# Head sums of an RWKV-7 layer: two rounded passes for one fp32 pass, and what moves with them

## The chip, the cores and the metric

The kernel runs on one core of a Trainium2 chip. The metric is the device time of one execution in microseconds (us), the median of the runs. TensorE (PE) multiplies, VectorE (DVE) and ScalarE (ACT) do the elementwise work, GpSimd (POOL) a little of it, and SyncE (SP) starts most of the DMA transfers.

## The reference

One layer of a hybrid decoder step: 1024 prompt tokens and 8 x 8 sample tokens, 1088 columns in all, model width 1024. `w_in` projects to RWKV-7 columns (14 blocks of 128), pooling columns (4 blocks) and gates (16 blocks). The sums over the 64 channels of a head are the three that the change touches:

```python
xl = pr + (pr_prev - pr) * lp["mu_shift"]                       # token shift
r, k, v, xw, xa, xg = jnp.split(xl, RWKV_SPLITS, axis=-1)
...
kk = heads(k * lp["k_k"])
kk = kk * lax.rsqrt(jnp.sum(kk * kk, axis=-1, keepdims=True) + 1e-12)
...
y, wkv_new = wkv7_scan(wkv_prev.astype(f32), rh, heads(decay), kh, vh, kk, ah)
mean = jnp.mean(y, axis=-1, keepdims=True)
var = jnp.mean(jnp.square(y - mean), axis=-1, keepdims=True)
y = ((y - mean) * lax.rsqrt(var + GN_EPS)).reshape(B, T, MIX_WIDTH)
y = y * lp["ln_w"].astype(f32) + lp["ln_b"].astype(f32)
bonus = jnp.sum(rh * kh * lp["r_k"].astype(f32), axis=-1, keepdims=True) * vh
y = (y + bonus.reshape(B, T, MIX_WIDTH)).astype(pr.dtype) * g
```

Then follow the causal pooling branch, the gated merge, `w_out`, and a squared-ReLU MLP (1024 to 4096 and back) between two adaptive norms.

## The kernel before

Channels lie on the 128 partitions, the 1088 tokens along the free dimension, cut in chunks (364, 362, 362 columns, or 512, 288, 288). The big products are done with a value split in two rounded halves (type fp32r): `hi` is a rounded copy made by ACT, `lo` the rest, subtracted by DVE, and three passes replace one fp32 product (`whi` and `wlo` are the halves of a weight, `hx` those of the activations). The small products of the heads are plain fp32.

The work of TensorE is one list, written out by hand when the program is built. `Pace.run` keeps an estimated TensorE clock. The stream `back` gives the weight products of the projection, a job for each block of `w_in`. The streams `fore` (chains of the state, heads, pools, the branch product's rows) are generators; each `yield n` says that its next step is to be put n estimated nanoseconds later, and until then products of `back` are put in between. The other engines' lists are made by a scheduler from the same program. Every engine runs its list in order. PSUM tag `w` has two banks used in turn, `mm` four, `wc` two; the SBUF ring `wt` has five buffers.

For each of four pairs of heads f (called head 0 to 3 here), `heads` runs: `front(f)` with the sample tokens of head f-1 beside it (`both` alternates two generators); `scores(f)`, in which the bonus follows the first unit; then `inverse`, `level` and `affine` (the 64 x 64 triangular inverse of each chunk) with `post(f-1)` beside them. At the end come `sample(3)` and `post(3)`.

- `front` squares k (ACT, L570), sums the squares over a head with a block matrix of ones (`kc("bones")`, an fp32 product in tag `w`), takes the inverse root in `rinv` (Sqrt on ACT at L332, reciprocals on DVE at L334 in pieces of at most 182 columns), and then the two decay products, each read by a Tanh (L582, L585). DVE does the rest (L602 to L627), and step by step the recurrent state S (L899).
- `scores` copies diagonal blocks with ACT (`iv`, L702).
- `post` is the group norm: a mean sum, its subtraction (L1004), a square (L1005), a second sum, `rinv`, scale and bias (L1011), bonus and gate (L1012, L1013). A gate product and its copy (L997) come first.
- `level` copies the products of the triangle from PSUM with DVE (L797, L808) and ACT (L812).
- `rwkv_cols` is the projection job of an RWKV block; its token shift is two DVE passes over the tile (L450, L452) and one over the sample tokens (L454). `gate` applies a Tanh to gate blocks (L471).
- The pool jobs add up windows with DVE (L508 to L521); `pools` multiplies the result by a 128 x 128 matrix (`plw`) and splits it (L548 on ACT, L549 on DVE).

An activation of another table set than the last is preceded by an ACT_TABLE_LOAD; Sqrt and Tanh are in different sets.

Of the kernel before, what the change touches and what calls it, by code (L numbers as in the profile page):

```python
# [18 lines left out]
P = 128  # L19
# [3 lines left out]
TS = 8  # L23
# [20 lines left out]
for _name, _w in (("ident", 128), ("ones", 128), ("bones", 128), ("strict", 64), ("incl", 64), ("strict8", 64), ("incl8", 64),  # L44
                  ("qm", 8), ("icnt", 16), ("one0", 9), ("par", 2), ("m16", 32), ("i32", 32), ("sel", 18)):
    KC[_name] = (_n, _w)
    _n += _w
# [3 lines left out]
def const_table():  # L51
    t = np.zeros((P, NKC), np.float32)

    def put(name, a):
        o, w = KC[name]
        t[:, o:o + w] = a

    r = np.arange(P)[:, None]
    put("ident", np.eye(P))
    put("ones", 1.0)  # L60
# [64 lines left out]
class K:  # L125
# [209 lines left out]

    def modulate(self, h, xn, g, am, kb, c0=0, n=NT, o=0):
# [87 lines left out]
    def rwkv_cols(self, b, act=None, tags=("mm", "mm", "mm")):  # L424
# [19 lines left out]
        def after():  # L444
# [5 lines left out]
            nc.vector.tensor_tensor(d[:, :1096], px[:, :1096], px[:, 1:1097], op=ALU.subtract)  # L450
            mu = self.par("mu", b)
            nc.vector.scalar_tensor_tensor(d[:, :NPR], d[:, :NPR], mu, px[:, 1:1 + NPR], op0=ALU.mult, op1=ALU.add)  # L452
            dv = d[:, 1025:1097].rearrange("p (q t) -> p q t", t=9)
            nc.vector.scalar_tensor_tensor(s.rearrange("p (q t) -> p q t", t=TS), dv[:, :, 0:8], mu, pv[:, :, 1:9],  # L454
# [76 lines left out]
    def pools(self):  # L531
# [3 lines left out]
        for g in range(4):  # L535
# [3 lines left out]
            yield 6500 + 1300 * g  # L539
# [16 lines left out]
    def front(self, f):  # L556
# [14 lines left out]
        t1, tha = self.wt(), self.wt()  # L571
        yield 8000 if f else 13000

        for c0, n in FP:
            ps = self.ps("w")
            self.mm(ps[:, :n], self.kc("bones"), kk[:, c0:c0 + n], start=True, stop=True)
            self.rinv(ps, n, kk[:, c0:c0 + n], 1.0, 1)
            yield 800
        for c0, n in FP:
# [19 lines left out]
        for c0, n in FH:  # L599
# [3 lines left out]
            nc.vector.tensor_tensor_scan(t, self.kscan[:, s], t, 0.0, ALU.mult, ALU.add)  # L603
# [19 lines left out]
        yield X(8 + f)  # L623
        v = self.wt()
        nc.sync.dma_start(v, self.d_x[8 + f])
        q = self.wt()
        nc.vector.scalar_tensor_tensor(q, r, self.par("r_k", f), k, op0=ALU.mult, op1=ALU.mult)  # L627
# [16 lines left out]
    def scores(self, f, d):  # L644
# [4 lines left out]
        yield from self.bonus(f, d)  # L649
# [3 lines left out]
    def bonus(self, f, d):  # L653

        nc, q, v, bv = self.nc, d["q"], d["v"], self.wt()
# [318 lines left out]
    def post(self, f):  # L974
# [9 lines left out]
        g2 = self.sm.tile([P, P], F32, tag="sw", bufs=2, name=self.nm("sw"))  # L984
        nc.sync.dma_start(g2, self.io["g2"][:, fs])
        sq = self.wt()
        bv = self.wt()
        nc.sync.dma_start(bv, self.d_bv[f])
        sg = self.wt()
        nc.sync.dma_start(sg, self.d_x[13])  # L990
        if not last:
            yield 5000

        for c0, n in CH:
            ps = self.ps("w")
            self.mm(ps[:, :n], g2, sg[:, c0:c0 + n], start=True, stop=True)
            nc.scalar.activation(sg[:, c0:c0 + n], ps[:, :n], AF.Copy)  # L997
            yield 500
# [29 lines left out]
        else:  # L1028
            live = [[piece(c0, n), self.pace.t + 700 * i] for i, (c0, n) in enumerate(CH)]
# [10 lines left out]
            hi, lo = self.row(self.p1, "wt", 5, F32R), self.row(self.p1, "wt", 5, F32R)  # L1040
            nc.scalar.activation(hi, y, AF.Copy)
            nc.vector.tensor_tensor(lo, y, hi.bitcast(F32), op=ALU.subtract)
# [4 lines left out]
    def heads(self):  # L1047

        for f in range(4):
# [8 lines left out]
            fill = self.post(f - 1) if f else self.ada_fill()  # L1058
            self.ds[f] = d

# [5 lines left out]
            yield from self.both(main(), fill)  # L1066
# [31 lines left out]
    def run(self):  # L1098
        tc, nc, io = self.tc, self.nc, self.io
        with ExitStack() as ctx:  # L1100
# [20 lines left out]
            nc.vector.tensor_scalar(self.hp[:, 12:16], self.hp[:, 8:12], -1.0, 1.0, op0=ALU.mult, op1=ALU.add)  # L1121
            self.sst = self.cp.tile([P, 14, 8], F32, name="sst")
# [21 lines left out]
    def phase1(self, ctx):  # L1144
# [27 lines left out]
        self.kscan = sm.tile([P, NT], BF16, name="kscan")  # L1172
        nc.gpsimd.memset(self.kscan, 1.0)
        nc.gpsimd.memset(self.kscan[:, 0:NPR:64], 0.0)
        nc.gpsimd.memset(self.kscan[:, NPR:NT:8], 0.0)
# [58 lines left out]
    def phase2(self):  # L1234
# [76 lines left out]
        gt = self.cp.tile([P, 8, 9], F32, name="gt1")  # L1311
        g2 = self.cp.tile([P, 8, 9], F32, name="g2")
# [460 lines left out]
    def residual(self, x, gt):  # L1773
        nc = self.nc

        def consume(c0, n, ps):
            m = min(n, NPR - c0)
            nc.vector.scalar_tensor_tensor(x[:, c0:c0 + m], ps[:, :m], gt[:, 0:1], x[:, c0:c0 + m], op0=ALU.mult, op1=ALU.add)
            if m < n:
                t = self.cp.tile([P, 64], F32, tag="rs", bufs=2, name=self.nm("rs"))  # L1780
# [109 lines left out]
```

## Time and profile before

| | |
|---|---|
| timed runs | 1677.7, 1677.36, 1667.94 us; median 1677.36 us |
| profiled execution | 1670.78 us, span 1669.0 us, mean granted clock 0.987 |
| PE, DVE, ACT, POOL busy | 1590.6, 1097.5, 638.2, 138.7 us |
| instructions | 35468 |
| heads and projections | about 60 to 812 us; merge and MLP after that |

A row of the timeline has the start, the length, engine, line, operation and operands, how many instructions are drawn together, and in brackets the idle time before them with what ended it. A row of grouped instructions has the shapes, the count, busy time, mean length in nanoseconds, idle time before and its causes. A row by stretch has for each engine busy time and count, then the granted TensorE clock, the DMA share and GB/s. In the waits stand total, times and longest.

### The profile page before, as it was taken

The page shows a single profiled execution, that of the slowest core. Times are in us where ns is not written, and L with a number is a line of the kernel's source. Part 1 is how long each engine was busy: PE and PEld are TensorE (multiplying, and loading weights), DVE is VectorE, ACT ScalarE, POOL GpSimd, SP SyncE. Part 2 cuts the span into 40 slices and gives each one's busy share as a digit, 9 for nine tenths or more (in the row PEclk, how much of TensorE's full clock was granted, in tenths as well). Part 3 has the DMA queues.
Part 4 walks back from the last instruction along what each step waited for, and adds up shares of the span by engine and source line. Part 5 has one row for each costly group of instructions (what it writes and reads, how often), then busy time and mean ns, then how long its engine had stood idle before and what let it go on. Part 6 is the DMA issues. An engine that isn't in the chain of part 4 may idle for free.

```text
span 1669.0 us, 35468 instructions
## 1 busy us (share of the span) xinstructions
PE 1590.6 (95%) x14619; PEld 1477.6 (89%) x14619; DVE 1097.5 (66%) x1911; ACT 638.2 (38%) x1249; POOL 138.7 (8%) x199
## 2 busy tenths in 40 slices
PE   4989999989897999999999999999999999999997
PEld 2878887887786879888999999999999999999997
DVE  4685658573859283824654479799866887566775
ACT  4443333343334333432222356222233434433651
POOL 0100101000000000000250130000000032000000
PEclk9999998999999999999999999999999999999999
DMA  9233312323241324175687456566434997665663
GB/s 350 81 101 137 137 60 78 116 77 113 88 137 44 134 75 147 54 276 180 220 307 274 150 182 217 184 236 212 161 141 151 364 365 256 200 212 163 213 197 121
DMA packets 121858, 288.37 MB, mean 173 GB/s; under 512 B 21120, under 2 KB 26752, under 8 KB 121696
## 3 DMA queue, kind: packets, MB, share of 16 engines
q1 hardware_dynamic: 113312, 264.65, 45.7%
q10 hardware_dynamic: 8240, 20.95, 3.6%
q8 instruction: 115, 1.88, 0.4%
q0 software_dynamic: 144, 0.51, 0.1%
q14 instruction: 47, 0.39, 0.1%
HBM read 208.77 MB, written 77.28 MB: 171 GB/s over the span
## 4 chain that ended last, share of the span: by engine, by line
PE 53%; DVE 6%; DMA 6%; issue 1%; ACT 1%; POOL 0%; SPq 0%; ACTq 0%; DVEq 0%; POOLq 0%
PE mm L156 36%; PE wc L156 10%; PE w L156 7%; DMA hid<-in_w_ff 1%; DVE wt L334 1%; DMA t<-d_t 1%; DMA mg<-in_w_ff 1%; DMA d_t<-hx 1%; DMA hid<-in_w_ada_mlp 1%; DVE wlo L1231 0%; DMA t<-d_th 0%; DVE hx L1582 0%; DVE hx L1466 0%; DMA wraw<-in_w_br 0%; DVE wlo L176 0%
## 5 line engine op out<-in xcount | busy, mean ns | idle before, releaser
L156 PE MATMUL mm<-hx,whi 128*128 128x362 f32 (+2 forms) x2944 | 708.5, 328 | 4.2 <-ACT px L471 1.5
L156 PEld LDWEIGHTS mm<-hx,whi 128*128 128x128 f32 x2944 | 499.7, 191 | 48.1 <-issue 22.1
L156 PE MATMUL mm<-hx,wlo 128*128 128x362 f32 (+2 forms) x1472 | 465.3, 316 | 1.8 <-DVE wlo L176 1.8
L156 PEld LDWEIGHTS mm<-hx,wlo 128*128 128x128 f32 x1472 | 281.0, 191 | 2.1 <-DVE wlo L176 2.1
L156 PE MATMUL mm<-mg,whi 128*128 128x272 f32 (+2 forms) x1312 | 248.8, 288 | 0.5 <-DVE t L1463 0.5
L156 PEld LDWEIGHTS mm<-mg,whi 128*128 128x128 f32 x1312 | 205.5, 188 | 5.1 <-issue 2.5
L156 PE MATMUL mm<-mg,wlo 128*128 128x272 f32 (+2 forms) x656 | 188.8, 288 | 0.0
L156 PE MATMUL wc<-hx,whi 128*128 128x272 f32 x896 | 169.5, 287 | 0.0
L156 PEld LDWEIGHTS wc<-hx,whi 128*128 128x128 f32 x896 | 140.3, 188 | 0.1
L1230 ACT ACTIVATE whi<-hid 128x512 fp32r<-128x512 f32 x128 | 80.4, 630 | 142.7 <-PE mm L156 59.6
L176 DVE TENSOR_TENSOR wlo<-wraw,whi 128x512 fp32r<-128x512 f32 x84 | 59.9, 714 | 113.5 <-ACT whi L175 109.5
L156 PE MATMUL wc<-hx,wlo 128*128 128x272 f32 x448 | 129.1, 288 | 1.1 <-DVE wlo L1231 1.1
L156 PEld LDWEIGHTS mm<-mg,wlo 128*128 128x128 f32 x656 | 123.5, 188 | 0.0
L1231 DVE TENSOR_TENSOR wlo<-hid,whi 128x512 fp32r<-128x512 f32 x128 | 88.0, 688 | 46.4 <-ACT whi L1230 45.7
L175 ACT ACTIVATE whi<-wraw 128x512 fp32r<-128x512 f32 x100 | 62.8, 629 | 138.8 <-PE mm L156 80.8
L156 PE MATMUL w<-hx,whi 128*128 128x272 f32 (+1 forms) x480 | 96.3, 295 | 0.0
L156 PEld LDWEIGHTS wc<-hx,wlo 128*128 128x128 f32 x448 | 84.3, 188 | 1.5 <-DVE wlo L1231 1.5
L1783 POOL TENSOR_TENSOR hx<-hx,rs 128x64 f32<-128x64 f32 x24 | 35.1, 1464 | 566.2 <-DMA mg<-in_w_ff 378.5
L156 PEld LDWEIGHTS mm<-mg,hx 128*128 128x128 f32 x576 | 72.7, 188 | 5.0 <-issue 5.0
L156 PEld LDWEIGHTS w<-hx,whi 128*128 128x128 f32 x480 | 77.0, 188 | 0.0
L156 PE MATMUL mm<-mg,hx 128*128 128x272 f32 (+2 forms) x576 | 75.4, 290 | 0.0
L156 PE MATMUL w<-hx,wlo 128*128 128x272 f32 (+1 forms) x240 | 70.9, 295 | 0.3 <-DVE wlo L1231 0.3
(324 smaller groups left out, 2350.0 us busy)
## 6 DMA issues: line engine op xcount, KB each, us to landing
t<-d_t SPq DMA_DIRECT2D x56, 544.0 KB, 4.7
hid<-in_w_ff SPq DMA_DIRECT2D x110, 256.0 KB, 3.7
d_t<-hx SPq DMA_DIRECT2D x102, 272.0 KB, 2.2
hid<-in_w_ff SPq DMA_DIRECT2D x42, 512.0 KB, 4.0
wraw<-in_w_in SPq DMA_DIRECT2D x68, 256.0 KB, 2.8
mg<-in_w_ff SPq DMA_DIRECT2D x58, 256.0 KB, 5.4
hid<-in_w_ada_mlp SPq DMA_DIRECT2D x24, 512.0 KB, 5.8
d_th<-px SPq DMA_DIRECT2D x22, 544.0 KB, 3.0
```

The lines of the kernel that those rows point to most:

```text
L156: return self.nc.tensor.matmul(out, lhsT, rhs, **kw)
L175: nc.scalar.activation(hi, raw, AF.Copy)
L176: (nc.gpsimd if n % 2 and n >= self.solo else nc.vector).tensor_tensor(lo, raw, hi.bitcast(F32), op=ALU.subtract)
L334: nc.vector.reciprocal(out[:, a:min(a + 182, n)], out[:, a:min(a + 182, n)])
L1230: self.nc.scalar.activation(hi, src, AF.Copy)
L1231: (eng or self.nc.vector).tensor_tensor(lo, src, hi.bitcast(F32), op=ALU.subtract)
L1783: nc.gpsimd.tensor_tensor(x[:, NPR:NT], x[:, NPR:NT], t, op=ALU.add)
```

## The change

- `halves` splits a value in hi (ACT copy) and lo (DVE subtract); `sums` adds up both with a rounded block matrix `bones`, in two fp32r passes. They replace the fp32 sums of kk and bonus for all heads and of the group norms of heads 0 to 2. `post(3)` keeps its fp32 sums.
- The kk sums stand 2000 estimated nanoseconds later.
- The bonus leaves `scores` and runs beside `inverse`, ahead of the post of the head before.
- In posts 0 to 2 the gate products come behind the sums, and bonus and gate are applied to the whole tile.
- The token shift is `px * mu + (1 - mu) * shifted`: a scaled copy on ACT for the second term and one DVE pass.
- The pools' waiting times are 6000 + 1000 g for 6500 + 1300 g. Constants and buffers not needed go (`ones`, half of `kscan`), and three small tiles of the second phase move to another pool.

```diff
+    def halves(self, src, hi, lo):
+        self.nc.scalar.activation(hi, src, AF.Copy)
+        self.nc.vector.tensor_tensor(lo, src, hi.bitcast(F32), op=ALU.subtract)
+
+    def sums(self, hi, lo):
+        ps = self.ps("w")[:, :hi.shape[1]]
+        for i, x in enumerate((hi, lo)):
+            self.mm(ps, self.bones, x, start=i == 0, stop=i == 1)
+        return ps
...
-            nc.vector.tensor_tensor(d[:, :1096], px[:, :1096], px[:, 1:1097], op=ALU.subtract)
-            nc.vector.scalar_tensor_tensor(d[:, :NPR], d[:, :NPR], mu, px[:, 1:1 + NPR], op0=ALU.mult, op1=ALU.add)
+            nc.scalar.activation(d[:, :1096], px[:, 1:1097], AF.Copy, scale=self.mu1[:, b:b + 1])
+            nc.vector.scalar_tensor_tensor(d[:, :NPR], px[:, :NPR], mu, d[:, :NPR], op0=ALU.mult, op1=ALU.add)
...
-            yield 6500 + 1300 * g
+            yield 6000 + 1000 * g
...
-        t1, tha = self.wt(), self.wt()
-        yield 8000 if f else 13000
+        hi, lo = (self.row(self.p1, "wt", 5, F32R) for _ in range(2))
+        for c0, n in FH:
+            self.halves(kk[:, c0:c0 + n], hi[:, c0:c0 + n], lo[:, c0:c0 + n])
+        yield 10000 if f else 15000
         for c0, n in FP:
-            ps = self.ps("w")
-            self.mm(ps[:, :n], self.kc("bones"), kk[:, c0:c0 + n], start=True, stop=True)
-            self.rinv(ps, n, kk[:, c0:c0 + n], 1.0, 1)
+            self.rinv(self.sums(hi[:, c0:c0 + n], lo[:, c0:c0 + n]), n, kk[:, c0:c0 + n], 1.0, 1)
             yield 800
...
         yield from self.unit(f, d, 0)
-        yield from self.bonus(f, d)
         yield from self.unit(f, d, 2)
...
-            ps = self.ps("w")
-            self.mm(ps[:, :n], self.kc("bones"), q[:, c0:c0 + n], start=True, stop=True)
-            nc.vector.tensor_tensor(bv[:, c0:c0 + n], ps[:, :n], v[:, c0:c0 + n], op=ALU.mult)
+            s = slice(c0, c0 + n)
+            nc.vector.tensor_tensor(bv[:, s], self.sums(hi[:, s], lo[:, s]), v[:, s], op=ALU.mult)
...
+            def part(c0, n):
+                s = slice(c0, c0 + n)
+                self.halves(y[:, s], hi[:, s], lo[:, s])
+                yield 2500
+                nc.vector.scalar_tensor_tensor(y[:, s], self.sums(hi[:, s], lo[:, s]), -1.0 / 64, y[:, s], op0=ALU.mult, op1=ALU.add)
+                nc.scalar.activation(sq[:, s], y[:, s], AF.Square)
+                self.halves(sq[:, s], hi[:, s], lo[:, s])
+                yield 5500
+                self.rinv(self.sums(hi[:, s], lo[:, s]), n, sq[:, s], 1.0 / 64, 2)
+                nc.vector.tensor_tensor(y[:, s], y[:, s], sq[:, s], op=ALU.mult)
+                nc.scalar.activation(y[:, s], y[:, s], AF.Identity, bias=self.par("ln_b", f), scale=self.par("ln_w", f))
...
+            bv, sg = yield from gate()
+            nc.vector.tensor_tensor(y, y, bv, op=ALU.add)
+            nc.vector.tensor_tensor(y, y, sg, op=ALU.mult)
...
-            fill = self.post(f - 1) if f else self.ada_fill()
+            def fill():
+                yield from self.bonus(f, d)
+                yield from self.post(f - 1) if f else self.ada_fill()
```

Line numbers shift by the edit: L332 becomes L331, L334 L333, L471 L482, L582 L595, L797 L809, L808 L820, L508 L519, L910 L922, L1004 L1052, L1010 L1057.

The first place is ACT's list in the front of head 3, from the Sqrt of the first kk sum to the first decay Tanh (`px` are gate blocks, `y` sample rows). Before:

```order
L332 ACT_TABLE_LOAD
L332 ACTIVATE wt_6177<-w_6254,eps 128x512
L332 ACTIVATE wt_6177<-w_6269,eps 128x288
L332 ACTIVATE wt_6177<-w_6280,eps 128x288
L910 ACTIVATE y_6303<-wc_6019 128x256
L582 ACT_TABLE_LOAD
L582 ACTIVATE wt_6181<-w_6294,hp 128x512
```

Of the change (without the rows ahead and the tanhs behind):

```order
L331 ACT_TABLE_LOAD
L331 ACTIVATE wt_6181<-w_6277,eps 128x512
L482 ACT_TABLE_LOAD
L482 ACTIVATE px_6120<-mm_6121 128x364
L482 ACTIVATE px_6120<-mm_6122 128x362
L922 ACTIVATE y_6334<-wc_6021 128x256
L331 ACT_TABLE_LOAD
L331 ACTIVATE wt_6181<-w_6296,eps 128x288
L174 ACTIVATE whi_6307<-wraw_6305 128x512
L482 ACT_TABLE_LOAD
L482 ACTIVATE px_6120<-mm_6123 128x362
L331 ACT_TABLE_LOAD
```

Gate tanhs now stand between the Sqrts, each with a load, and one more Sqrt, a copy and a load follow before the first decay Tanh.

The second place is DVE's list in `post(1)`, beside `inverse` and `level` of head 2, around the reciprocals of the second sum (`hv` are products of the triangle, `px` and `d` pool 3's tiles). Before:

```order
L518 SCALAR_TENSOR_TENSOR px_5286<-px_5465,px_5286 128x1024
L334 RECIPROCAL wt_5372<-wt_5372 128x182 x2
L519 COPY px_5286<-zf_5478 128x15
L797 TENSOR_TENSOR hv_5629<-w_5564,kct 128x512
L334 RECIPROCAL wt_5372<-wt_5372 128x182
L334 RECIPROCAL wt_5372<-wt_5372 128x180
L1010 TENSOR_TENSOR wt_5368<-wt_5368,wt_5372 128x364
L334 RECIPROCAL wt_5372<-wt_5372 128x182
L334 RECIPROCAL wt_5372<-wt_5372 128x180
L1010 TENSOR_TENSOR wt_5368<-wt_5368,wt_5372 128x362
L549 SCALAR_TENSOR_TENSOR px_5465<-w_5655,part,d_5464 128x364
```

Of the change:

```order
L338 TENSOR_TENSOR wt_5404<-wt_5402,wt_5403 128x362 x2
L809 TENSOR_TENSOR hv_5597<-w_5532,kct 128x512
L333 RECIPROCAL wt_5402<-wt_5402 128x182 x3
L333 RECIPROCAL wt_5402<-wt_5402 128x180
L333 RECIPROCAL wt_5402<-wt_5402 128x182
L333 RECIPROCAL wt_5402<-wt_5402 128x180
L1057 TENSOR_TENSOR wt_5400<-wt_5400,wt_5402 128x364
L1057 TENSOR_TENSOR wt_5400<-wt_5400,wt_5402 128x362
L820 COPY hv_5739<-w_5642 32x512 x2
L1057 TENSOR_TENSOR wt_5400<-wt_5400,wt_5402 128x362
L175 TENSOR_TENSOR wlo_5755<-wraw_5752,whi_5754 128x512
L519 TENSOR_TENSOR d_5766<-px_5418 128x1038
```

The first product's step stands ahead of all reciprocals instead of behind two; the copy of the second comes behind all six; the pool's adds, which before came ahead of this piece, begin behind it.

More of the change, by code (lines that the diff above doesn't have):

```diff
@@ L1039, in post @@
                     live.remove(x)
-            hi, lo = self.row(self.p1, "wt", 5, F32R), self.row(self.p1, "wt", 5, F32R)
-            nc.scalar.activation(hi, y, AF.Copy)
-            nc.vector.tensor_tensor(lo, y, hi.bitcast(F32), op=ALU.subtract)
+            bv, sg = yield from gate()
+            nc.vector.tensor_tensor(y, y, bv, op=ALU.add)
+            nc.vector.tensor_tensor(y, y, sg, op=ALU.mult)
+            hi, lo = (self.row(self.p1, "wt", 5, F32R) for _ in range(2))
+            self.halves(y, hi, lo)
             nc.sync.dma_start(self.d_or[0][f], hi.bitcast(F32))
@@ L1064, in main @@
                 yield from self.affine(f, d)
-            yield from self.both(main(), fill)
+            yield from self.both(main(), fill())
         yield from self.sample(3, d)
```

66 lines of the change are left out of this document (38 added, 28 removed).

## The prediction

> **What bounds the kernel now.** I read the page first, then busy time by stretch, then what TensorE (PE) waits for in the part that the change touches.
>
> ```profile
> PE 1590.6 (95%) x14619; PEld 1477.6 (89%) x14619; DVE 1097.5 (66%) x1911; ACT 638.2 (38%) x1249; POOL 138.7 (8%) x199
> ```
>
> PE is busy for 95% of the span, so an instruction taken off PE is worth its length only if PE does not then stand still for it. How long it does so in the first phase is in the sum of the busy times by stretch, from 60 to 830 us:
>
> ```profile
> sum 770.00, PE 728.45 PEld 641.73 DVE 470.09 ACT 285.90 POOL 58.83; mean PE 56.03 PEld 49.36 DVE 36.16 ACT 21.99 POOL 4.53
> ```
>
> PE idles 770.00 - 728.45 = 41.6 us there. The waits of the same stretch name whom it waits for:
>
> ```profile
> PE wc L156 <- DVE S L899: 7.2, 3, 3.9
> PE w L156 <- DVE hv L797: 4.8, 3, 2.1
> PE w L156 <- ACT iv L702: 4.4, 5, 1.4
> PE w L156 <- DVE px L549: 4.3, 3, 2.9
> PE w L156 <- ACT wt L570: 4.3, 1, 4.3
> ```
>
> All of these are steps of the heads and pools, whose VectorE (DVE) or ScalarE (ACT) partner comes late. The change removes work on PE in just these steps and gives DVE and ACT more to do there. So I count what PE saves, then each place where its partner gets later.
>
> **PE work removed.** The price of a sum is read in the dense stream:
>
> ```profile
> 136.58 0.33 PE L156 MATMUL mm<-hx,wlo 128*128 128x362 f32 x1
> 136.75 0.77 PE L156 MATMUL w<-wt,kct 128*128 128x364 f32 x2
> 137.08 0.78 PE L156 MATMUL mm<-hx,whi 128*128 128x362 f32 x2
> 137.70 0.33 PE L156 MATMUL mm<-hx,wlo 128*128 128x362 f32 x1
> 137.86 0.33 PE L156 MATMUL mm<-hx,whi 128*128 128x364 f32 x1
> ```
>
> A rounded pass over 362 columns takes 137.86 - 137.70 = 0.16 to 0.17 us (starts, not the modelled ends). From wlo to wlo are 1.12 us, which hold three such passes (0.50) and the fp32 sum: 0.62 us. Two passes take 0.33, so a chunk saves 0.29 and a whole sum of 1088 columns 0.88 us. Fourteen are changed (four kk, four bonus, six in posts 0 to 2): 12.4 us. The kk sums of heads 1 to 3 (2.7 us) stand in fronts in which PE waits for others afterwards; I give them no gain of their own, since the terms for those fronts below are counted from wait to wait. That leaves **-9.7 us**. (Head 0's kk sum is behind a 4.27 us wait for the square, L570; its sum now stands 12 products, 2.0 us, later in PE's order, as long as the added copy and subtract take by the rows below, so the wait stays.)
>
> **ACT and DVE work added and moved.**
>
> ```profile
> L1041 ACT ACTIVATE wt<-wt 128x1088 fp32r<-128x1088 f32 x3 | 3.3, 1111 | 2.6 <-DVE wt L1013 2.6
> L1042 DVE TENSOR_TENSOR wt<-wt,wt 128x1088 fp32r<-128x1088 f32 x3 | 3.9, 1293 | 3.0 <-ACT wt L1041 3.0
> L450 DVE TENSOR_TENSOR d<-px 128x1096 f32<-128x1096 f32 x14 | 18.1, 1293 | 0.8 <-ACT iv L702 0.6 <-POOL ns L447 0.2
> L332 ACT ACT_TABLE_LOAD x8 | 10.3, 1283 | 3.7 <-issue 3.1 <-PE w L156 0.5
> ```
>
> Halves: 14 x 1.11 = 15.5 us on ACT, 14 x 1.29 = 18.1 us on DVE. The token shift gives DVE 14 x 1.29 = 18.1 us back and costs ACT as much as a copy of that length, 16 us. DVE's total thus stands still, ACT gets 31 us on 286 in 770: neither becomes a bound on average. What counts is place. ACT also gets six more table loads, because in the new order a gate's or the shift's tanh stands between Sqrts: two in head 1's front, four in head 3's.
>
> *Fronts.* Today's:
>
> ```profile
> 241.08 1.28 ACT L332 ACT_TABLE_LOAD   x1
> 242.40 0.69 ACT L332 ACTIVATE wt<-w,eps 128x512 f32<-128x512 f32 x1
> 245.85 0.38 ACT L910 ACTIVATE y<-wc 128x256 f32<-128x256 f32 x1
> 246.24 1.28 ACT L582 ACT_TABLE_LOAD   x1
> 247.57 0.69 ACT L582 ACTIVATE wt<-w,hp 128x512 f32<-128x512 f32 x1
> 245.45 0.50 ACT L332 ACTIVATE wt<-w,eps 128x288 f32<-128x288 f32 x1 [0.98 <-PE w L156]
> L471 ACT ACTIVATE px<-mm 128x362 f32<-128x362 f32 x32 | 15.0, 469 | 2.1 <-PE mm L156 1.9
> ```
>
> One load serves three Sqrts and runs while PE still sums. In head 3's front ACT must now do, from the end of the first sum (0.5 us after its start): load 1.28, Sqrt 0.69, load, two gate tanhs 0.94, a copy 0.38, load, second Sqrt 0.50 (6.9 us); a weight copy of 512 columns (at most the 0.69 of a Sqrt of that width), load, tanh 0.47, load, third Sqrt (11.1); copy, load, first decay tanh (13.4). PSUM tag w has two banks, so PE's first decay product needs the second Sqrt done, the next the third, the one behind it the first tanh. PE's own work to that product is 4.4 us (26 passes); each product of 512 columns is at most 0.9 by the 0.62 above. So it waits 2.5, 3.3 and 1.4 us. The waits of today in that front go:
>
> ```profile
> 595.77 0.33 PE L156 MATMUL w<-x,z 64*64 64x64 f32 x4 [0.18 <-ACT wt L582]
> 602.61 0.33 PE L156 MATMUL w<-ab,uv 128*64 128x64 f32 x2 [0.58 <-ACT wt L582]
> 617.36 0.33 PE L156 MATMUL wc<-S,ra 64*64 64x64 f32 x4 [1.01 <-DVE S L899]
> ```
>
> 7.2 - 1.8 = **+5.4** for head 3. Heads 1 and 2 wait for S at the end of theirs:
>
> ```profile
> 272.68 0.33 PE L156 MATMUL wc<-S,ra 64*64 64x64 f32 x4 [2.21 <-DVE S L899]
> 440.65 0.33 PE L156 MATMUL wc<-S,ra 64*64 64x64 f32 x4 [3.95 <-DVE S L899]
> 120.27 0.48 PE L156 MATMUL w<-ra,bk 64*128 64x128 f32 x2 [0.75 <-ACT iv L702]
> ```
>
> Head 1's front has two loads and the shift's tanh between its first and second Sqrt, which puts them 3 to 4 us later; it ends on DVE today (2.21), whose reciprocals start later but which no longer does L450 there: +1. Head 2's front gets pool 1's three products between its kk sums, whose PSUM is released by DVE behind the reciprocals: about 5.5 us of waits for the 3.95 that go, +1.5. Fronts **+8**, from 0 (the loads run ahead of PE after all) to +12 (all six loads, 7.7 us, on the path, and the pool).
>
> *Scores.* The copy of q's upper half (1.11) and the shift's multiplication come ahead of the copies L702, for which PE waits 4.4 us in all today, 0.75 at 120.27: **+1** (0 to +3).
>
> *Posts, beside inverse and level.* The first two rows are head 1's, the third head 3's, the next three head 2's, the last three PE's small products and DVE's:
>
> ```profile
> 362.77 1.29 PE L156 MATMUL w<-wt,kct 128*128 128x362 f32 x2 [2.14 <-DVE hv L797]
> 370.97 0.32 PE L156 MATMUL w<-hv,iv 32*32 32x32 f32 x9 [1.70 <-issue]
> 700.90 1.50 PE L156 MATMUL w<-wt,kct 128*128 128x362 f32 x2 [2.14 <-DVE hv L797]
> 524.31 0.88 PE L156 MATMUL w<-wt,kct 128*128 128x362 f32 x2 [2.09 <-DVE wt L1004]
> 538.79 1.20 PE L156 MATMUL w<-hv,iv 32*32 32x32 f32 x64 [2.87 <-DVE px L549]
> 543.42 1.57 PE L156 MATMUL w<-px,plw 128*128 128x362 f32 x2 [3.43 <-ACT z L812]
> 528.72 1.29 PE L156 MATMUL w<-hv,hv 32*32 32x32 f32 x128
> 521.14 1.24 DVE L508 TENSOR_TENSOR d<-px 128x1038 f32<-128x1038 f32 x1
> 535.43 2.42 DVE L334 RECIPROCAL wt<-wt 128x182 f32<-128x182 f32 x2
> ```
>
> Head 2 loses 8.4 us by these rows, head 1 3.8, head 3 2.1; some small ones of half a microsecond stand beside them, so I take 9.5, 4.3 and 2.4. Now the copy of the triangle's product (L797, L809 after) stands ahead of the six reciprocals, so the 2.14 goes. But the copy of the next product (L808, L820 after) comes behind all six: 6 x 1.21 + 0.5 + 1.4 for itself = 9.2 us after the first Sqrt, 11.5 after the first sum of squares began with the weight subtract ahead of it, and the second gate product needs its bank. PE's own work from that sum to the gate product: 18 passes 3.0, six of the sums 1.0, 96 small products 1.9 (64 of them, two records each, take 1.29), one gate product 0.62: 6.5. So head 1 waits about 5.0 (+0.7), head 3, without the subtract, 4.3 (+1.9). In head 2 pool 3 moves behind all this: four adds (5.0), four short ones 1.4, y's bonus, gate and subtract (3.9), 1.8 for the pool's last, 1.5 for y, 0.7 for weights, with 8.7 for reciprocals and copies some 23 us, less overlaps and with the 2 before the first Sqrt again 23, against 13.2 of PE work up to pool 3's first product: 9.8 of waits (+0.4). Sum **+3** (from -6, if DVE starts earlier than I assume or the pool's product finds it done, to +8).
>
> *Clock.*
>
> ```profile
> 540.00:550.00 10.00, 6.58 (x37) 5.69 (x39) 6.28 (x11) 5.28 (x8) 0.00 (x0) 0.66 0.54 158
> 360.00:370.00 10.00, 7.12 (x199) 5.77 (x199) 9.96 (x14) 3.15 (x6) 0.00 (x0) 0.83 0.12 34
> ```
>
> Behind 2.87 and 3.43 us of waiting the granted clock is 0.66 for 10 us, behind 2.14 it is 0.83: 3.4 and 1.7 us at most. Two or three more waits of that size than today, and less of the 0.66: **+1** (-2 to +4).
>
> **Sum.** -9.7 + 8 + 1 + 3 + 1 = +3.3 us on the profiled execution's 1670.78 us (span 1669.0 and 1.8 around it): 1674. The three timed runs are 1667.94, 1677.36 and 1677.7, their median 7 above the profiled one; I stay at the sum. Phase two and the end of phase one I cost at nothing: the heads end some 11 us earlier in PE's order, but the first store it waits for is that of the gate tanhs.
>
> **A rule of the Trainium skill.** The loads' row says 1.28 us, and 245.85 + 0.38 to 247.57 is 1.34 from one activation to the next across a switch. The Trainium skill, "ScalarE: Activation LUTs", section "What ACT_TABLE_LOAD costs", adds a drain of about 1.38 us, 2.66 in all; it also advises doing all of one set before switching, which this order breaks. By that page head 3's front would come out some 5 us longer and the sum 1679; the trace shows no drain here.
>
> **Rivals.** *The saving comes through*: scheduling around the sums hides what is added, because DVE's total is unchanged and the posts' new order takes the pool out of the triangle. Then -12.4, with the posts' waits 4 us shorter and the fronts at 0: 1655 to 1661, say 1659. For it: the 8.4 us of waits around 540 that can go; against it: four loads that cannot run ahead of a Sqrt. Chance 0.25. *DVE's queue decides*: each head's post and front puts its pieces behind six reciprocals, and PE waits for the gate's bank and the pool's product. If copies come another 2 us later than I count in each of three posts (+6), and the fronts cost their upper price (+4), clock +3: 1674 + 13 = 1687. It begins where DVE reaches the copy more than 5 us after PE reaches the gate product. Chance 0.17. *A gap at each switch*: if every load of head 3's front stood still as long again as it takes (1.28), four times on the path: 1679, where the quoted 1.34 from end to start speaks against it; 0.03. The page named above gives such a gap. *The passes are no shorter in place*, because the two halves arrive one after the other and PE takes the second only when DVE is done: the saving goes, 1684; the order gives each sum 2 us or more for it: 0.05. The forecast has 0.5.
>
> **Range and chances.** 1656 to 1688 takes in the first rival and nearly all of the second. About 1% (17 us) is what a measurement of this kernel tells from no change: against the median 1677.36 faster means under 1661, slower over 1694. Half of the first rival lies under that, with a little of the forecast's lower bounds: 0.14; of the others little lies over: 0.07; the rest is within.
>
> **What would show it.** Right: 25 table loads; PE waiting 2 us or more three times in head 3's front behind L331 and L595; waits of 3 us or more at the second gate product of heads 1 to 3 behind L820, and at pool 3's first product behind L529; PE's busy time some 12 us less and its idle time some 15 more. Wrong: idle time in 60 to 830 us at 41 or less would make it faster, by the 10 us. If PE's waits do rise, but elsewhere, the sum was luck.

## The result, and the profile after

The change takes 1695.99 us (median of 6 runs, 1688.74 to 1698.58), the kernel before 1675.58 beside it (6 runs): a ratio of 1.0122 [1.0095, 1.0148], 20 us slower. The forecast was 1674 and the range ended at 1688. The profiled execution took 1695.66 us (span 1693.6) against 1670.78; the one of before lies 5 us below its median, so differences of a few us between the two traces are scatter. The granted clock of every timed run is on record too: 0.987 in the trace of before and 0.981 to 0.989 (median 0.984) in the 92 runs of it that were timed beside r1 to r18; 0.971 to 0.978 (median 0.973) in the six of the change, 0.975 in its trace.

Busy time on the page, to be held against the same line of before:

```profile
PE 1603.0 (95%) x14619; PEld 1492.5 (88%) x14619; DVE 1093.9 (65%) x1916; ACT 675.1 (40%) x1299; POOL 123.7 (7%) x200
```

The number of PE's instructions is the same and the sums of 42 chunks are shorter, yet PE is busy 12.4 us *longer*. The page's line of the granted clock, before and after, says where to look:

```profile
PEclk9999998999999999999999999999999999999999
```
```profile
PEclk9999998999999979998999999999999999999999
```

The digits below 9 in slices 15 and 19 are new. So I divide the first phase, from 60 us to the first product with the sample states (`wc<-hid,sT`, at 858.9 us before and 882.3 after), into three parts. Its row by stretch has length, PE's busy time, the other engines, then the granted clock. Before, then after:

```profile
60.00:858.90 798.90, 757.35 (x8057) 670.39 (x8055) 488.05 (x862) 294.61 (x621) 74.89 (x130) 0.98 0.37 126
```
```profile
60.00:882.30 822.30, 767.03 (x8057) 682.70 (x8055) 485.54 (x866) 331.51 (x671) 62.15 (x132) 0.95 0.36 123
```

**Idle** is the length less PE's busy time: 41.5 and 55.2 us (from stretches of 2 us, which the row agrees with). **Clock** is busy time multiplied by what the granted clock lacks of 1, summed over those stretches: 16.4 and 35.5 us (the two digits of the rows give 757 x 0.02 = 15 and 767 x 0.05 = 38). **Work** is what is left: 741.0 and 731.5. Of the 23.4 us, idle time is +13.7, the clock **+19.1** and work -9.5; behind the phase come 1.2 more. The timed runs bear the clock's part out: 0.984 less 0.973, of some 1600 us in which PE is busy, is an estimated 18 us.

By place, cut at whole microseconds (so that the columns add up to the totals only within 1.1 us):

| place | idle before, after | clock before, after |
|---|---|---|
| front of head 0 | 4.3, 6.1 | 2.9, 1.7 |
| fronts of heads 1 to 3 | 9.0, 16.1 | 8.4, 18.7 |
| scores | 5.4, 8.9 | 0, 3.2 |
| inverse of head 0 | 0, 4.4 | 0, 2.2 |
| inverse and posts 0 to 2 | 22.1, 13.7 | 5.2, 5.1 |
| behind the heads | 1.8, 6.6 | 0, 4.6 |

The costliest waits of PE after (total, times, longest):

```profile
PE w L155 <- issue: 8.1, 4, 2.6
PE w L155 <- ACT wt L331: 6.6, 6, 3.0
PE mm L155 <- DVE px L1257: 5.9, 3, 3.3
PE w L155 <- ACT iv L714: 4.9, 4, 1.6
PE w L155 <- ACT wt L595: 4.4, 6, 1.2
```

No wait in this phase is longer than 3.9 us, but the clock is at half (0.50; such a stretch is called a dip from here on) in 14 stretches instead of 8, each 3.5, 7 or 10.5 us long to within the half microsecond in which I read them. Four of them by stretch after, in heads 1, 1, 2 and 3:

```profile
254.00:264.00 10.00, 8.17 (x102) 6.91 (x101) 8.59 (x14) 3.74 (x8) 0.00 (x0) 0.66 0.27 98
264.00:274.00 10.00, 10.00 (x65) 8.22 (x65) 6.58 (x11) 2.27 (x5) 0.00 (x0) 0.66 0.21 66
416.00:426.00 10.00, 8.88 (x85) 6.33 (x85) 7.91 (x12) 3.36 (x8) 0.00 (x0) 0.66 0.22 89
594.00:604.00 10.00, 6.71 (x40) 3.94 (x40) 7.42 (x11) 6.86 (x11) 0.00 (x0) 0.57 0.27 98
```

The second has PE busy for all of its 10 us and still loses a third of the clock.

### The profile page after: what moved, and what is told of

It reads as the page before. It is cut to its first block, busy times and chain, and to the rows that moved or that the text cites. A ratio compares the mean times of both kernels' runs of the same rounds, so it can differ in the third digit from the quotient of the medians.

```text
span 1693.6 us, 35581 instructions
## 1 busy us (share of the span) xinstructions
PE 1603.0 (95%) x14619; PEld 1492.5 (88%) x14619; DVE 1093.9 (65%) x1916; ACT 675.1 (40%) x1299; POOL 123.7 (7%) x200
## 4 chain that ended last, share of the span: by engine, by line
PE 58%; DMA 4%; DVE 4%; issue 1%; ACT 1%; POOL 0%; SPq 0%; ACTq 0%; DVEq 0%; POOLq 0%
PE mm L155 38%; PE wc L155 12%; PE w L155 8%; DMA hid<-in_w_ff 1%; DMA hid<-in_w_ada_mlp 1%; DMA d_th<-px 1%; DMA wraw<-in_w_br 1%; DMA mg<-in_w_ff 1%; DVE wt L333 0%; DMA t<-d_th 0%; DMA wt<-d_x 0%; DVE hx L1622 0%; DVE wlo L175 0%; POOL wlo L175 0%; DVE wlo L1271 0%
```

## The experiments

All are timed beside the kernel before, whose medians were 1674.0 to 1675.84. Idle, clock and work are those of the first phase, counted as above, from one profiled execution each.

| kernel | us | ratio | idle | clock | work |
|---|---|---|---|---|---|
| before | | 1 | 41.5 | 16.4 | 741.0 |
| the change | 1695.99 | 1.0122 [1.0095, 1.0148] | 55.2 | 35.5 | 731.5 |
| r1 change, one more yield of 2500 | 1678.00 | 1.0021 [1.0007, 1.0034] | 44.9 | 29.4 | 729.3 |
| r2 change, kk yields of before | 1697.23 | 1.0139 [1.0115, 1.0164] | 55.4 | 39.9 | 729.9 |
| r3 change, bonus in `scores` | 1698.14 | 1.0157 [1.0128, 1.0187] | 62.5 | 29.0 | 730.0 |
| r4 change, posts of before | 1689.28 | 1.0102 [1.0077, 1.0126] | 48.5 | 23.3 | 737.4 |
| r5 before, kk sums of the change | 1685.59 | 1.0076 [1.0053, 1.0098] | 49.9 | 22.7 | 737.2 |
| r6 before, bonus of the change | 1689.91 | 1.0095 [1.0074, 1.0116] | 43.7 | 32.3 | 739.9 |
| r7 before, posts of the change | 1687.82 | 1.0084 [1.0061, 1.0107] | 50.4 | 25.9 | 737.1 |
| r8 before, token shift of the change | 1671.65 | 0.9986 [0.9969, 1.0003] | 44.1 | 11.1 | 742.4 |
| r9 before, kk, bonus, posts 0, 1 in place | 1678.19 | 1.0017 [1.0003, 1.0031] | 49.5 | 22.0 | 729.9 |
| r10 r9 and the token shift | 1680.96 | 1.0030 [1.0016, 1.0044] | 57.0 | 17.8 | 731.9 |
| r11 before, kk yields of the change | 1683.88 | 1.0047 [1.0029, 1.0066] | 47.6 | 20.7 | 742.4 |
| r12 before, one more yield of 2500 | 1671.56 | 0.9973 [0.9960, 0.9986] | 36.8 | 23.4 | 740.5 |
| r13 before, kk and bonus in place | 1677.11 | 1.0016 [1.0001, 1.0030] | 45.8 | 24.3 | 733.7 |
| r14 r8 and r12 | 1672.55 | 0.9984 [0.9973, 0.9996] | 33.0 | 22.0 | 741.0 |
| r15 r13, shift and yield | 1673.39 | 0.9993 [0.9982, 1.0004] | 39.8 | 26.0 | 735.1 |
| r16 change, one more yield of 5000 | 1687.71 | 1.0077 [1.0062, 1.0091] | 53.6 | 31.2 | 731.5 |
| r17 r13, each sum twice | 1697.00 | 1.0132 [1.0108, 1.0156] | 52.6 | 25.5 | 741.7 |
| r18 change, each sum twice | 1707.00 | 1.0169 [1.0127, 1.0212] | 52.2 | 31.3 | 745.5 |

### Which piece of the change costs: r1 to r4

r1, in `front`, behind the loop over the kk sums of heads 1 to 3, lets PE's other stream go on for an estimated 2500 ns:

```diff
             yield 800
+        if f:
+            yield 2500
```

> Change plus one line: 2500 estimated ns more of weight products between the kk sums and the first decay product of heads 1 to 3; ACT's list then has 21 table loads, and the three Sqrts of head 3's front stand together. Theory A (most of the loss is in the fronts: waits behind the table loads, and behind each cluster of waits 3.4 to 7 us at half clock): the fronts of heads 1 to 3 lose some 15 us less, 1681 to 1687. Theory B (the loss is in the posts and the inverse, DVE behind its reciprocals): 1694 to 1698. Theory C (the two-pass sums are no shorter in place): 1694 to 1698. Theory D (the heads' earlier end, which puts the last norm onto the branch products): a little better, 1692, as the heads end later.

r2 puts the sums back to their old place in time:

```diff
-        yield 10000 if f else 15000
+        yield 8000 if f else 13000
```

> Change with the kk sums at 13000 and 8000 ns as before it, 2000 earlier than in the change; 21 table loads, head 3's Sqrts together, head 1's still parted by the shift's tanh. Theory A: front 3 gives back 8 to 10 us, front 0 costs 2 more because its sum waits for the halves: 1687 to 1690. Theory B and C: 1695 to 1699. Theory D: heads end still earlier, 1697 to 1700.

r3 takes the bonus back from beside the inverse into `scores`:

```diff
         yield from self.unit(f, d, 0)
+        yield from self.bonus(f, d)
         yield from self.unit(f, d, 2)
...
             def fill():
-                yield from self.bonus(f, d)
```

> Change with the bonus back between units 0 and 2 of the scores, in two passes. 21 table loads. Theory A: the loads alone give 6 to 8 us, the scores lose 2 to 4: about 1691. Theory B: the inverse loses three DVE multiplications per head: 1690 to 1694. Theory D: the heads end later, the end of phase one loses some 8 us less, and together with the inverse of head 0 (4 us) the time is 1682 to 1686.

r4 has the posts of before, with fp32 sums:

```diff
-            live = [[part(c0, n), self.pace.t + 700 * i] for i, (c0, n) in enumerate(CH)]
+            live = [[piece(c0, n), self.pace.t + 700 * i] for i, (c0, n) in enumerate(CH)]
...
-            bv, sg = yield from gate()
-            nc.vector.tensor_tensor(y, y, bv, op=ALU.add)
-            nc.vector.tensor_tensor(y, y, sg, op=ALU.mult)
```

> Change with the posts of before: gate products first, fp32 sums, bonus and gate applied in pieces. 21 table loads. Theory B: the posts were the loss, 1680 to 1686. Theory A: sums cost 5.3 us more and the waits beside the inverse rise again by 8, while the fronts lose 8 less: 1695 to 1702. Theory C: 1690 to 1694, as the fp32 sums cost nothing more.

One line, which removes nothing, gives back 17 of the 20 us (1.0122 to 1.0021): idle -10.3, clock -6.1. r1 to r4 each have 21 table loads for the change's 25, and r2 and r3 are no faster than the change, so the loads alone are not what costs. Undoing the posts takes 18.9 us off idle time and clock and puts 5.9 of work back; the timed ratio falls by only 0.0020, and the intervals overlap. The trace is the mildest of r4's four runs (1684.46 us at a clock of 0.983; the others 1687.66 to 1693.62 at 0.979 to 0.973), so the 18.9 is more than r4 gives as a rule. For r1 it is the other way round: the clock of its ten runs is 0.979 to 0.982, median 0.981, so that by the medians (0.008 of some 1600 us) an estimated 13 of the 17 us are the clock's, not 6.1.

### Each part alone on the kernel before: r5 to r8

The four edits are pieces of the change's diff; "..." marks lines left out. r5, the kk sums:

```diff
-        yield 8000 if f else 13000
...
+            self.halves(kk[:, c0:c0 + n], hi[:, c0:c0 + n], lo[:, c0:c0 + n])
+        yield 10000 if f else 15000
...
+            self.rinv(self.sums(hi[:, c0:c0 + n], lo[:, c0:c0 + n]), n, kk[:, c0:c0 + n], 1.0, 1)
```

> Kernel before with only the kk sums of the change (halves, two passes, 15000 and 10000 ns); 19 table loads as before. If the parts' costs add up and the fronts' loss comes from the kk sums: +5 to +10 over before. Theory A (loss is in how the parts fall together in the fronts, not in a part): within 3 of before, as three of four sums stand where the front waits anyway. Theory C (two passes no shorter): +2 to +4 from copies and subtracts.

r6, the bonus with its two passes, beside the inverse:

```diff
-        yield from self.bonus(f, d)
...
+                yield from self.bonus(f, d)
+                yield from self.post(f - 1) if f else self.ada_fill()
```

> Kernel before with only the bonus of the change (two passes, beside the inverse); 21 table loads. Work 3.5 us less. Theory A: any shift of the heads against the projections changes which tanh stands between Sqrts, so waits and clock can take 5 to 10 back: +2 to +8. Without such a shift: -3. Theory D (heads' earlier end hurts): +3 to +6 in the last 100 us.

r7, posts 0 to 2:

```diff
+            live = [[part(c0, n), self.pace.t + 700 * i] for i, (c0, n) in enumerate(CH)]
...
+            bv, sg = yield from gate()
```

> Kernel before with only the posts of the change (sums in two passes, gate behind them); 19 table loads. Theory B: +6 or more. Theory A: work -5.3 and the waits beside inverse and level -8 as seen in the change: -8 to -13. Theory C: -8 from the waits alone.

r8, the token shift:

```diff
-            nc.vector.tensor_tensor(d[:, :1096], px[:, :1096], px[:, 1:1097], op=ALU.subtract)
...
+            nc.scalar.activation(d[:, :1096], px[:, 1:1097], AF.Copy, scale=self.mu1[:, b:b + 1])
```

> Kernel before with only the token shift of the change (scaled copy on ACT, one DVE pass); 19 table loads, TensorE's order unchanged. If ACT's place in the scores and fronts counts: +2 to +5, from the copies behind which TensorE waits. If DVE's relief counts more (fronts end on DVE): -2 to -4.

Each of the three that touch sums costs 11 to 16 us by itself, though each takes work off PE (by -3.8, -1.1 and -3.9 here); the token shift costs nothing that can be told from zero. The four sum to +38 (11.3 + 15.7 + 13.6 - 2.6), all together to +20: they are not prices that add up.

### The place or the passes: r9 to r12

r9 has the two passes for kk, bonus and posts 0 and 1 at the places in PE's order that the fp32 sums had, by charging PE's estimate as before. It has neither the token shift nor the change's waiting times, post 2 keeps its fp32 sums, and posts 0 and 1 apply bonus and gate to the whole tile as the change does:

```diff
+        t = self.pace.t + (0 if self.mode == (P, P) else 200)
+        for i, x in enumerate((hi, lo)):
+            self.mm(ps, self.bones, x, start=i == 0, stop=i == 1)
+        self.pace.t = t + hi.shape[1] / 0.6 + 3
```

> Kernel before with the sums of kk, bonus and posts 0 and 1 in two passes (12 of the change's 14), each standing exactly where its fp32 pass stood: the builder's clock charges the two passes as one fp32 pass, and all waiting times are those of before, so TensorE's list is the old one with each sum replaced. Work 10.6 us less. Theory A (the passes save, and the displaced order loses it): 5 to 10 us under before, 1664 to 1669. Theory C (passes no shorter in place, or copies and subtracts eat it): before or up to 4 above. Theory B (DVE behind its reciprocals): +3 to +6, since DVE gets 15 us more.

r10 adds the token shift to it:

```diff
+            nc.scalar.activation(d[:, :1096], px[:, 1:1097], AF.Copy, scale=self.mu1[:, b:b + 1])
```

> As the same-order kernel, with the token shift of the change as well. If the shift's 2.6 us add up: 2 to 3 under it, 1661 to 1666. If ACT's extra 16 us come ahead of the added copies: equal or up to 4 above.

r11 is a placebo: the kernel before, all of its sums in fp32, with only the waiting times of kk changed.

```diff
-        yield 8000 if f else 13000
+        yield 10000 if f else 15000
```

> Kernel before with the kk sums' waiting times alone changed, 15000 and 10000 for 13000 and 8000; no instruction is added or removed but for table loads (21 for 19). Theory A: +4 to +12, from displacement alone. Theories B and C: within 3 of before.

r12 is the kernel before with the line of r1:

```diff
+        if f:
+            yield 2500
```

> Kernel before with the line that mended the change (2500 ns more between kk sums and decay products of heads 1 to 3). If fronts simply want more products between sums and decay: -5 to -10. Theory A, by which the line mended one displaced order and displaces another: 0 to +10.

The placebo costs 8 us (1683.88 against 1675.22) without one pass or copy changed: idle +6.1, clock +4.3 (its list has two table loads more, 21 for 19, which the new order brings). So up to 8 of r5's 11 are the new place. With all twelve sums in their old places (r9) the whole of the slowdown but 3 us is gone, and the work is 11.1 us less; but nothing is gained, since idle and clock together take 13.6 back. The largest wait of r9 is one of 10.6 us. The timelines of PE and of DVE there:

```profile
539.74 1.55 PE L155 MATMUL w<-px,plw 128*128 128x364 f32 x2 [10.60 <-issue]
```
```profile
533.44 2.41 DVE L333 RECIPROCAL wt<-wt 128x182 f32<-128x182 f32 x2
...
537.13 1.22 DVE L531 SCALAR_TENSOR_TENSOR px<-px,px 128x1024 f32<-128x1024 f32 x1
...
539.47 0.16 DVE L532 COPY px<-zf 128x15 f32<-128x15 f32 x1
```

PE stands at pool 3's first product until 539.74; DVE finishes its operand `px` at 539.63, behind the reciprocals of post 1. This is the mechanism of the rival "DVE's queue decides"; the trace names "issue", but DVE's list shows what was late. r12 is faster than both kernels (1671.56, 0.9973): the extra yield does not need the change.

### Two passes in place, and the best of the pieces: r13 to r16

r13 is r9 without the posts; its `front` and `bonus`:

```diff
+        for c0, n in FH:
+            self.halves(kk[:, c0:c0 + n], hi[:, c0:c0 + n], lo[:, c0:c0 + n])
         yield 8000 if f else 13000
...
+            nc.vector.tensor_tensor(bv[:, s], self.sums(hi[:, s], lo[:, s]), v[:, s], op=ALU.mult)
```

> Kernel before with the kk and bonus sums in two passes (8 sums), each where its fp32 pass stood, posts as before: DVE's list keeps pool 3's work ahead of post 1's reciprocals. Work 7 us less. If displaced order and DVE's reciprocals are all that took the saving away: 2 to 5 under before (bonus 3.5 of work, kk largely behind the fronts' waits, head 0's sum 1 to 1.5 later for its halves), 1670 to 1673. If the passes or the halves eat it: before or slower.

r14 is the kernel before with the token shift of r8 and the yield of r12, r15 is r13 with both:

```diff
+            nc.scalar.activation(d[:, :1096], px[:, 1:1097], AF.Copy, scale=self.mu1[:, b:b + 1])
...
+        if f:
+            yield 2500
```

> Kernel before with the token shift of the change and the 2500 ns line, no sums changed. If the two small gains (0.9986 and 0.9973) add: 6 to 7 under before, 1668. If the one's order takes the other's: 1670 to 1675.

> Kernel before with kk and bonus in two passes at their old places, the token shift and the 2500 ns line. If all add: 9 to 12 under before, 1663 to 1666. If the sums bring nothing in place: as the kernel without them, 1668 to 1670.

r16 is r1 with a longer yield:

```diff
+        if f:
+            yield 5000
```

> Change with 5000 instead of 2500 ns between sums and decay products; 25 table loads again. If it was the amount of products that mended the fronts: equal to the 2500 kernel or better, 1674 to 1680. If it was how the lists then fall together (21 loads and one trio of Sqrts in head 3): back up, 1685 to 1697.

In r13 the eight sums save their 7.3 us of work, and 4.3 of idle time and 7.9 of clock come back (by the medians of the timed runs, 0.982 against 0.984, the clock's part is an estimated 3). The waits that grew most are for ACT, which now makes the upper halves as well:

```profile
PE w L155 <- ACT iv L717: 5.6, 5, 2.7
PE w L155 <- ACT z L848: 5.6, 2, 4.3
PE w L155 <- ACT wt L337: 5.5, 1, 5.5
```

4.4, 1.8 and 4.3 us before. The chip gave nothing for the shorter passes even in place. r16 gives back only 7 of the 20 (1.0122 to 1.0077): 2500 is not the start of a trend, it is one order among others. r14 and r15 do not beat r12.

### Does PE's time in the sums count at all: r17, r18

Every sum is computed twice into the same bank, PE's estimate as before; the second result is the same. r17 is r13 so, r18 the change:

```diff
+        for _ in range(2):
+            for i, x in enumerate((hi, lo)):
+                self.mm(ps, self.bones, x, start=i == 0, stop=i == 1)
```
```diff
+        t = self.pace.t
+        for i, x in enumerate((hi, lo)):
+            self.mm(ps, self.bones, x, start=i == 0, stop=i == 1)
+        self.pace.t = t
```

> The kernel with kk and bonus in two passes at their old places, with each of its 8 sums made twice (the second overwrites the first with the same values): 24 pairs of passes, 8 us of TensorE work, put back at those places; the builder's clock is not charged for them. If the saved work is lost to TensorE's waits and its clock there, putting it back costs next to nothing: within 3 of 1677, ratio 1.000 to 1.004. If TensorE's work there sets the time and the halves' lateness took the saving away: +6 to +8, 1683 to 1685.

> The change with each of its 14 sums made twice, 14 us of TensorE work more at the same places. Waits and clock take it up: 1693 to 1700. Work counts: 1706 to 1711.

r17 has 8 us more work on PE than r13 and is 19 slower (1.0132 against 1.0016); in the idle time are +6.8, in the clock +1.2. DVE's and ACT's lists had also changed a little, so the 19 is not the price of passes alone, but it refutes the idea that PE's time in these sums is free. r18 adds 14.0 of work and is 8 slower in ratio, with intervals that overlap: no more than that it is not faster.

Eight of the eighteen runs (r1, r3, r4, r5, r6, r12, r15 and r17) came out at a time that no theory in their expectations held. That the order counts is shown by the runs; how much a given order costs was not foretold.

## Why the prediction was wrong, point by point

**The passes.** Right in the price of a sum, and in part lucky in the total. The step forecast -9.7 of work, measured is -9.5; but the measured figure holds all fourteen sums, which the prediction priced at 12.4, while its 9.7 leaves out three of the kk sums. In place a sum saves 0.91 us (r13, 7.3 for eight) and 0.93 (r9, 11.1 for twelve), where 0.88 was forecast; r8 and r11, which change no sum, still have 1.4 more work than before, so one or two us of such a difference is scatter. The two-pass rows after, and the fp32 rows of before of the same two shapes (8 of the 48 and 4 of the 24 are post 3's, which stay):

```profile
L155 PE MATMUL w<-wt,bones 128*128 128x362 f32 x40 | 9.8, 346 | 1.2 <-DVE wt L1052 1.2
L155 PE MATMUL w<-wt,bones 128*128 128x364 f32 x20 | 4.9, 328 | 0.0
```
```profile
L156 PE MATMUL w<-wt,kct 128*128 128x362 f32 x48 | 20.0, 506 | 7.8 <-DVE hv L797 4.3 <-DVE wt L1004 2.1 <-ACT wt L332 1.5
L156 PE MATMUL w<-wt,kct 128*128 128x364 f32 x24 | 9.3, 468 | 0.0
```

Each chunk has two records in both, of 346 ns now for 506, so the rival "passes no shorter in place" is out.

**The fronts.** Right in sum: +8 forecast, +7.1 of idle time in heads 1 to 3. In head 3 ACT did what the step counted, with the six loads; its timeline behind the first Sqrt, and PE's:

```profile
589.32 1.28 ACT L482 ACT_TABLE_LOAD   x1
590.61 0.84 ACT L482 ACTIVATE px<-mm 128x364 f32<-128x364 f32 x2
591.75 1.28 ACT L331 ACT_TABLE_LOAD   x1
593.04 0.50 ACT L331 ACTIVATE wt<-w,eps 128x288 f32<-128x288 f32 x1
...
597.16 0.50 ACT L331 ACTIVATE wt<-w,eps 128x288 f32<-128x288 f32 x1
```
```profile
591.14 0.60 PE L155 MATMUL mm<-hx,whi 128*128 128x362 f32 x2 [0.82 <-ACT px L482]
...
593.60 1.12 PE L155 MATMUL w<-wt,sw 64*128 64x512 f32 x2 [1.21 <-ACT wt L331]
597.71 2.07 PE L155 MATMUL w<-wt,sw 64*128 64x512 f32 x2 [2.99 <-ACT wt L331]
600.08 0.48 PE L155 MATMUL w<-x,z 64*64 64x64 f32 x4 [0.30 <-ACT wt L595]
```

1.21, 2.99 and 0.30 us stand where 2.5, 3.3 and 1.4 were forecast. ACT came when the step said: from the start of the first sum at 586.60, the second Sqrt ends after 6.9 us, the third after 11.1 and the first tanh after 13.3 (6.9, 11.1 and 13.4 forecast). PE came later: it was at the first product 5.8 us after that start and not 4.4, having stood 0.82 us for a gate tanh, which the step did not have, and the product ahead of the third took 2.07 us at half clock, where 0.9 at most was counted. A switch takes 1.29 from the load's start to the activation's (589.32 to 590.61), with no gap, so the rival "a gap at each switch" is out; the drain of 1.38 us that the Trainium skill, "ScalarE: Activation LUTs", section "What ACT_TABLE_LOAD costs", adds is not in this trace. The 25 loads were as forecast.

**The scores.** +1 (0 to +3) forecast, +3.5 of idle time and 3.2 of clock: just above the bound.

**Posts, inverse, level.** Too high: +3 (-6 to +8) forecast, -8.4 measured beside posts 0 to 2. The waits at the gate's second product and at the pool, forecast at 3 us and more and near 10:

```profile
536.91 1.00 PE L155 MATMUL w<-wt,sw 128*128 128x362 f32 x2 [2.65 <-DVE hv L820]
549.07 0.85 PE L155 MATMUL w<-px,plw 128*128 128x364 f32 x2 [1.08 <-issue]
556.40 0.88 PE L155 MATMUL w<-px,plw 128*128 128x362 f32 x2 [3.11 <-ACT at L861]
```

Heads 1 and 3, for which 5.0 and 4.3 were forecast at the second gate product, wait 0.52 us and not at all. So "DVE's queue decides", whose 1687 came nearest in time, was not what happened in the change; r9 shows that its mechanism exists. Two places that the sum had at nothing ate the gain, with +4.4 and +4.8 of idle time. In the inverse of head 0 PE waits in the middle of runs of 32x32 products:

```profile
194.79 1.09 PE L155 MATMUL w<-iv,hv 32*32 32x32 f32 x106 [1.81 <-issue]
198.79 1.38 PE L155 MATMUL w<-hv,iv 32*32 32x32 f32 x44 [2.58 <-issue]
```

Of the four waits named "issue" (8.1 us) three stand in such runs; the third, of 2.62 us, is at 707.30. In the first gap no engine was late: between 193 and 194 us DVE, ACT and POOL have no record at all. In r1 and r2 PE stands at the same two products (1.01 and 2.03 us, 0.18 and 2.86), 128 products apart. The page's DMA queue "instruction" (q8) moved 115 packets for PE's 2 x 14619 records, one for 254 of them. So PE may have waited there for its own instructions; that is not shown, and no run was made for it. And behind the heads, where I had written that the first store was early enough, DVE's part of a branch comes late, at the end of a chain through a store and a reload of `px`, for which ACT stands 7.23 us, then post 3's Sqrt and two reciprocals:

```profile
794.24 0.97 PE L155 MATMUL mm<-hx,whi 128*128 128x362 f32 x2 [3.34 <-DVE px L1257]
```
```profile
789.46 1.28 ACT L331 ACT_TABLE_LOAD   x1 [7.23 <-DMA d_th<-px]
```

In total idle time came to +13.7, for the 15 named under "what would show it". The sum of these terms was nearly right, by errors that cancel, and with it "the saving comes through" is out: the idle time it needed away was there.

**The clock: the step that failed.** +1 (-2 to +4) forecast, +19.1 measured. With 19.1 in its place the sum is 1670.78 - 9.7 + 8 + 1 + 3 + 19.1 = 1692.2, beside the profiled 1695.66. I priced it from the stretches behind two waits of 2.9 and 3.4 us and one of 2.14, as if only a wait of 2 us or more brought a dip. Of such waits the phase has eight before and seven after; of dips it has 8 and 14. The trace of before already held the counter-examples, which I had quoted without looking at the clock behind them: the wait of 2.09 at 524.31 brings none, and the 0.58 at 602.61, among the sample tokens' small products, is followed by half clock from 605.5 on:

```profile
522.00:536.00 14.00, 10.67 (x291) 7.97 (x290) 13.91 (x23) 6.02 (x10) 2.50 (x5) 1.00 0.09 26
```
```profile
604.00:614.00 10.00, 10.00 (x72) 7.73 (x73) 9.95 (x18) 3.76 (x9) 1.45 (x2) 0.83 0.26 99
```

After, there is one with no wait at all. Some 30 products of 64x8 go by, and behind a pass of 364 columns with a record of 0.33 us one of 362 takes 0.51:

```profile
764.17 0.92 PE L155 MATMUL w<-ra,hv 64*64 64x8 f32 x13
...
765.92 0.33 PE L155 MATMUL mm<-hx,wlo 128*128 128x364 f32 x1
...
766.61 0.51 PE L155 MATMUL mm<-hx,wlo 128*128 128x362 f32 x1
```

The two traces together have these sample products eight times: behind a wait of 0.58 us a dip followed each of five times, without one it followed once in three. That speaks for the wait, but neither it nor the small products decide it alone, and what does is open. Where PE is busy a dip costs half its length, 1.7 us for each 3.5, whatever brought it; the change has six more. The lengths agree with the Trainium skill, "TensorE: Matmul & The Clock Gate", section "Part 1: The HAM clock gate (the "warmup" mystery)", by which half rate follows an idle window of about 3.4 us that runs free; that it takes a whole window of idle time is not what these traces show, since a dip came with PE busy. The clock's share is accounted for from one profiled execution of each kernel, and borne out by the clocks of the timed runs; no run changed the clock and nothing else. The nearest to it are the change's own six runs, the same program each time: 1688.74 us at 0.978, 1698.58 at 0.971, where 0.007 of some 1600 us is an estimated 11. The sign "PE's busy time some 12 us less" failed with this step: a pass that takes 0.33 us in its record takes 0.51 at half clock, and the busy time came out 12.4 longer.

**Why the order costs that much.** Shown: displacing the kk sums with no change of work costs 8 us (r11), one yield gives back 17 (r1), a yield twice as long 7 (r16), and the same passes in their old places are within 3 us of before (r9, r13). So the loss lies in how the change's pieces fall between the main stream's products, and the passes themselves, in place, are neither a cost beyond those 3 us nor, in the end, a gain. That the kernel before sits in an unusually good order, so that nearly any displacement loses, is argued from this and not shown; r12, which is faster than it by 3.7 us, says that the order was not the best.

## What to carry to other kernels

Split a stretch into idle time, time lost to the granted clock and work before pricing a change, and look at the clock behind short waits among small products too: there 0.58 us of waiting was followed by a dip five times of five, and the dip cost more than the wait. Before a part of a change is credited or blamed, run its displacement alone, without the part; here the placebo was 8 us and a single yield 17, where 12 were to be saved. Work that is taken off a saturated engine is only gained if its partners are not later, and a scheduler's order has to be set again after the edit. One trace is one run: hold its clock against those of the timed runs before reading a few us out of it.

## What was not expected of the hardware

- Half clock (0.50 granted) came in stretches of 3.5, 7 or 10.5 us, behind waits of 0.58 us and at 766 us behind none, where PE was fully busy with 64x8 and 64x64 products; waits of 1.31, 1.44, 1.78 and 2.09 us (at 126.65, 326.40, 385.35 and 524.31 us of before) brought none, two of them ahead of 64x64 products. In r9 one stretch lasts 14 us, around the wait of 10.60.
- In this kernel that costs 11 to 40 us in 800 (between 11.1 in r8 and 39.9 in r2), and 29.4 or 39.9 for the same products in two orders (r1, r2).
- A wait named "issue" can hide an engine: 10.60 us in r9, in which DVE was working on the operand. It can also fall where no engine is at work: 1.81 us at 194.79 of the change.
